# First loads dealt over two queues, 20 warming products in place of 27, and the input's squares in four wide pinned instructions, in a hybrid decoder layer

## The chip, the core and the metric

The kernel runs on one core of one Trainium2 chip. The metric is the device time of one execution in microseconds (us). Three runs of the kernel before took 1563.19, 1560.8 and 1563.22 us; their median is 1563.19 us. The profile was taken from one more execution of 1562.6 us, whose span from the first instruction to the last is 1560.7 us.

## The reference

The kernel computes one layer of a decoder on 256 tokens of width 2048, in float32, with weights read from memory:

```python
u = rms_norm(h, pre_mix_gain, 1e-6)          # u = x * rsqrt(mean(x*x) + eps) * gain
z = u @ w_in                                 # 2048 x 14336
zq, zk, zv, zc, zga, zgc = split(z)
...                                          # differential attention on zq, zk, zv
zc = zc + glu_bias
c_val, c_gate = split(zc, 2)
c = c_val * sigmoid(c_gate)
c = causal_depthwise_conv(c, dw_kernel, dw_bias)     # 31 taps
c = silu(layer_norm(c)); conv_out = c @ w_conv_out + b_conv_out
m = sigmoid(zga) * attn_out + sigmoid(zgc) * conv_out
h = h + rms_norm(m @ w_out, post_mix_gain)
f = square(relu(rms_norm(h, pre_ff_gain) @ w_ff1)) @ w_ff2
return h + rms_norm(f, post_ff_gain)
```

The first norm matters here. The factor rsqrt(mean(x*x) + eps) is one number per token, so it can be applied behind the product with `w_in`: the kernel multiplies x by the gain alone, starts the products, and scales the sums later.

## The kernel before

**Chunks.** All weights come in chunks of 128 x 2048 float32 (1 MiB), in one fixed order: first the 32 chunks of the convolution branch, in pairs of one value chunk (`w_cv`) and one gate chunk (`w_cg`), then q, k, v, the gates, the output projections and the feed-forward layer. Each chunk is loaded into a buffer `raw` (three buffers) by a DMA that SyncE issues (line 97), rounded to a high half `wh` by ScalarE (line 103) and to a low half `wl`, raw minus `wh`, by VectorE (line 109). `wh` and `wl` have three buffers each, so a chunk's halves can be written once TensorE has done with those of the chunk three places before. A `raw` buffer is free for its next load when the chunk's `wl` is written.

**Products.** TensorE works through a pair of chunks in `ws_pair`: for each chunk 16 products of `wh` with the activations' two halves side by side (512 columns, line 180), then 16 of `wl` with the high half (256 columns, line 182). A pair fills one of two PSUM tiles `ps`. ScalarE copies one part of the sum out (line 187) into `z`, VectorE adds the rest (line 188), and then the PSUM tile is free for the pair after the next. `z` has two buffers.

**The lead.** The first pair (chunks 0 and 1, raw tiles `lead[0]` and `lead[1]`) is done in pieces, so that TensorE can start early: x (2 MiB, transposed, tile `xt`) and the two chunks are loaded in parts, and for each of four groups j of four k-tiles ScalarE writes the high halves of x times gain (line 157) and of the weights, VectorE the low halves (lines 158 and 109), and TensorE does lines 168 and 171 for each k-tile and chunk. All this is pinned in the written order. Before it TensorE runs `WARM` products of the identity with itself (line 293), which leave no result.

**The norm's factor.** Lines 325 to 341 square x (ScalarE, 16 instructions of 128 x 256), add the squares up in `xss` (VectorE, 15 additions), sum over partitions with a product with ones (lines 336 and 340, on TensorE), and take square root and reciprocal: `rb` (per column) and `rt` (per token). `xt` and `xss` live in a pool that is closed behind this. `rb` is needed when the first pair's `z` is scaled (line 384); behind that come the sigmoid (line 385), the gated value `c` (line 388) and the filter (lines 369 and 373). The third pair's `z` can be written only when the first pair's `c` is done, since `z` has two buffers.

**Order.** Instructions that are pinned (`pin`) keep the written order among themselves; the rest are placed on each engine by a scheduler that estimates a timeline and takes priorities (`tc.high_priority`). At run time each engine runs its own list strictly in order, and waits on semaphores where an operand isn't there. A DMA signals on one of eight counters in turn, so the ninth one waits for the landing of the one that had its counter.

Of the kernel before, what the change touches and what calls it, by code (L numbers as in the profile page):

```python
# [11 lines left out]
F32 = mybir.dt.float32  # L12
F32R = mybir.dt.float32r
AF = mybir.ActivationFunctionType
ALU = mybir.AluOpType
# [3 lines left out]
P = 128  # L19
S = 256  # L20
NT = S // P
D = 2048
KT = D // P
# [16 lines left out]
CONV_LATE = 4000  # L40
CHAIN = 400
CHAINS = 2
WARM = 27
AHEAD = 3
LAG = 4
EARLY = 3
# [6 lines left out]
def tile_layer(ctx, tc, x, x_t, pre, vecs, lams, rope_t, subln, b_conv, post_mix, post_ff,  # L53
               w_q, w_k, w_v, w_cv, w_cg, w_ga, w_gc, w_co, w_o, w_f1, w_f2, out):
    nc = tc.nc
# [25 lines left out]
    pin = tc.keep_in_program_order  # L81

    def load(pieces):
        i = state["next"]
        state["next"] += 1
        state["live"] += 1
        chunk = (rawp.tile([P, CHUNK], F32, name="raw"), whp.tile([P, CHUNK], F32R, name="wh"),
                 wlp.tile([P, CHUNK], F32R, name="wl"))
        for j in range(pieces):
            load_part(chunk, i, j, pieces)  # L90
        queue.append(chunk[1:])
        return chunk

    def load_part(chunk, i, j, pieces, pinned=False, eng=None):
        w = CHUNK // pieces
        sl = slice(j * w, (j + 1) * w)
        a = (eng or nc.sync).dma_start(chunk[0][:, sl], order[i][:, sl])
        if pinned:
            pin(a)
# [117 lines left out]
    def rsqrt(dst, src, eps_tile, scale=1.0):  # L217
        nc.scalar.activation(dst, src, AF.Sqrt, bias=eps_tile, scale=scale)
        nc.vector.reciprocal(dst, dst)
# [4 lines left out]
    def aux_ps():  # L224
        tag = XT[xi[0] % 4]
        xi[0] += 1
        return psx.tile([P, 512], F32, name="aux", tag=tag)
# [30 lines left out]
    xsp = xst.enter_context(tc.tile_pool(name="xsp", bufs=1))  # L258
    xt = xsp.tile([P, KT, S], F32, name="xt")
    gpre = const.tile([P, KT], F32, name="gpre")  # L260
    lead = [load(0) for i in range(2)]

    def load_x(a, b):
        pin(nc.sync.dma_start(xt[:, a:b], x_t[:, a:b]))

    load_x(0, 2)
    pin(nc.scalar.dma_start(gpre, pre))
    load_part(lead[0], 0, 0, 4, pinned=True)
    load_part(lead[1], 1, 0, 4, pinned=True, eng=nc.scalar)
    load_x(2, 4)  # L270
    for j in range(1, 4):
        load_x(4 * j, 4 * j + 4)
        load_part(lead[0], 0, j, 4, pinned=True)
        load_part(lead[1], 1, j, 4, pinned=True, eng=nc.scalar)
    epsn = const.tile([P, 1], F32, name="epsn")
    nc.vector.memset(epsn, NORM_EPS)
    warm = const.tile([P, 1], F32, name="warm")
# [3 lines left out]
    ones = const.tile([P, P], F32, name="ones")  # L281
# [9 lines left out]

    for i in range(WARM):
        pin(nc.tensor.matmul(aux_ps()[:, 0:P], ident, ident, start=True, stop=True))
# [28 lines left out]
    def vcol(ct, r):  # L322
        return vec[:, ct, r:r + 1]

    xss = xsp.tile([P, S], F32, name="xss")
    for k in range(KT):
        if k == 0:
            nc.scalar.activation(xss, xt[:, k], AF.Square)
        else:
            sq = xsp.tile([P, S], F32, name="xsq", bufs=2)  # L330
            nc.scalar.activation(sq, xt[:, k], AF.Square)
            nc.vector.tensor_tensor(xss, xss, sq, op=ALU.add)
    rb = const.tile([P, S], F32, name="rb")
    rt = const.tile([P, NT], F32, name="rt")
    pb = aux_ps()[:, 0:S]
    nc.tensor.matmul(pb, ones, xss, start=True, stop=True)
    rsqrt(rb, pb, epsn, 1.0 / D)
    pc = aux_ps()[:, 0:NT]
    for t in range(NT):
        nc.tensor.matmul(pc[:, t:t + 1], xss[:, t * P:(t + 1) * P], ones[:, 0:1], start=True, stop=True)  # L340
    rsqrt(rt, pc, epsn, 1.0 / D)
    xst.close()
    rb2 = rb.unsqueeze(1).to_broadcast([P, 2, S])

# [160 lines left out]
    for j in range(4):  # L505
        yj = y_all[:, 4 * j:4 * j + 4]
        nc.vector.tensor_tensor(yj, yj, acc1.unsqueeze(1).to_broadcast([P, 4, S]), op=ALU.subtract)
        for ct in range(4 * j, 4 * j + 4):
            if ct == 0:
                nc.scalar.activation(acc2, y_all[:, ct], AF.Square)  # L510
            else:
                sq = tmpp.tile([P, S], F32, name="sq")
# [24 lines left out]
    for n in range(NB):  # L537
# [7 lines left out]
        for j in (2 * n, 2 * n + 1):  # L545
            pt = aux_ps()
            for i in range(2):
                k = 2 * j + i
# [19 lines left out]
    for n in range(NB):  # L568
        ps = as_block(ma, apart=(n == NB - 1))
        ns = slice(n * 512, (n + 1) * 512)  # L570
        with tc.high_priority(offset=CHAIN if n == NB - 1 else 0):
            for t in range(NT):
                sq = fin2.tile([P, 512], F32, name="fsq")
# [61 lines left out]
    for q in range(NQ):  # L635
# [9 lines left out]
        for n in range(NB):  # L645
            ps = as_block(ga, stagger=(q == NQ - 1 and n == NB - 1), apart=(q == NQ - 1 and n == NB - 1))
            ns = slice(n * 512, (n + 1) * 512)
            for t in range(NT):
# [5 lines left out]
                if q == NQ - 1:  # L654
                    last = n == NB - 1
                    with tc.high_priority(offset=CHAIN if last else 0):
                        sq = fin2.tile([P, 512], F32, name="fsq")
# [81 lines left out]
```

## Time and profile before

| what | value |
|---|---|
| median of three runs | 1563.19 us (1560.8 to 1563.22) |
| profiled execution | 1562.6 us, span 1560.7 us |
| TensorE (PE) busy | 1543.0 us, 99% of the span |
| VectorE (DVE) busy | 1118.0 us, 72% |
| ScalarE (ACT) busy | 719.7 us, 46% |
| TensorE's mean granted clock | 0.995 of full speed |
| DMA | 296.86 MB, mean 190 GB/s |

TensorE is busy nearly all the time, and the chain of work that ended last is TensorE for 97% of the span. So time can be taken from this kernel only where TensorE idles or runs at the lower clock, and those places are few; the list of what TensorE waited for shows them, and the timelines of the first 65 us show what stands around them. "PEld" is TensorE's loading of weights, which runs beside its products; a float32 product appears as two records.

### The profile page before, as it was taken

Reading aid. Unit: us, or ns where it says so; the run is one execution under the profiler, and the core shown is the slowest. Engines: PE = TensorE matmul, PEld = TensorE weight load, DVE = VectorE, ACT = ScalarE, POOL = GpSimd, SP = SyncE. Lnnn points to the kernel's source line nnn. Section 1 sums busy time; section 2 is a strip of 40 time slices with the busy share of each in tenths; the row PEclk is TensorE's granted clock in tenths of the full one; section 3 lists DMA queues with packets and bytes.
Section 4 is the critical chain, followed back from the end, with each engine's and each line's share of the span. In section 5 each row is a group of like instructions: output and inputs, shape, how many; then the busy total and the mean of one; then the engine's idle time right before and its main releaser. Section 6 shows DMA issues by size and latency. Waiting matters only on the chain.

```text
span 1560.7 us, 19198 instructions
## 1 busy us (share of the span) xinstructions
PE 1543.0 (99%) x7844; PEld 1319.0 (85%) x7844; DVE 1118.0 (72%) x1409; ACT 719.7 (46%) x755; POOL 5.2 (0%) x28
## 2 busy tenths in 40 slices
PE   9999999999999999999999999999999999999997
PEld 8788888888888888888887888888888888888886
DVE  7899999999999997956546764456554665456554
ACT  7444454645555545733435543444433443344442
POOL 0000000000000000000000000000000000000000
PEclk9999999999999999999999999999999999999999
DMA  7555555454545555555654654555555555555552
GB/s 286 195 191 189 189 189 188 165 187 162 189 162 185 195 197 195 196 187 182 266 193 147 234 189 175 200 199 189 188 190 194 190 189 185 191 211 189 174 200 84
DMA packets 45143, 296.86 MB, mean 190 GB/s; under 512 B 5120, under 2 KB 5248, under 8 KB 10368
## 3 DMA queue, kind: packets, MB, share of 16 engines
q1 hardware_dynamic: 43632, 289.34, 51.3%
q0 software_dynamic: 704, 5.24, 0.8%
q10 hardware_dynamic: 720, 1.06, 0.2%
q8 instruction: 61, 1.00, 0.2%
q14 instruction: 26, 0.21, 0.0%
HBM read 293.53 MB, written 2.10 MB: 189 GB/s over the span
## 4 chain that ended last, share of the span: by engine, by line
PE 97%; DVE 1%; DMA 1%; ACT 0%; issue 0%; DVEq 0%; ACTq 0%
PE ps L180 29%; PE ps L197 16%; PE ps L198 16%; PE ps L196 16%; PE ps L182 15%; PE ps L168 1%; DMA raw<-in_w_cv_dram 1%; PE po L456 1%; PE ps L171 1%; PE s L428 0%; PE aux L197 0%; PE aux L196 0%; PE aux L198 0%; DVE y_sb L672 0%; PE aux L236 0%; PE s L427 0%
## 5 line engine op out<-in xcount | busy, mean ns | idle before, releaser
L109 DVE TENSOR_TENSOR wl<-raw,wh 128x2048 fp32r<-128x2048 f32 (+2 forms) x292 | 625.3, 2145 | 376.4 <-ACT wh L103 372.0
L103 ACT CAST wh<-raw 128x2048 fp32r<-128x2048 f32 (+2 forms) x292 | 522.2, 1793 | 717.6 <-PE ps L198 342.2
L180 PE MATMUL ps<-act,wh 128*128 128x512 f32 x1984 | 480.5, 393 | 3.6 <-DVE z L188 3.6
L180 PEld LDWEIGHTS ps<-act,wh 128*128 128x128 f32 x1984 | 365.7, 189 | 74.4 <-issue 3.7
L182 PEld LDWEIGHTS ps<-act,wl 128*128 128x128 f32 x1984 | 256.5, 191 | 10.0
L182 PE MATMUL ps<-act,wl 128*128 128x256 f32 x1984 | 264.0, 284 | 0.0
L196 PE MATMUL ps<-wh,act 128*128 128x512 f32 x624 | 243.7, 391 | 0.0
L198 PE MATMUL ps<-wh,act 128*128 128x512 f32 x624 | 243.7, 390 | 0.0
L197 PE MATMUL ps<-wl,act 128*128 128x512 f32 x624 | 243.5, 390 | 0.0
L373 DVE SCALAR_TENSOR_TENSOR y_all<-c,vec,y_all 128x256 f32<-128x256 f32 x480 | 209.9, 482 | 0.0
L196 PE MATMUL ps<-wh,g 128*128 128x512 f32 x496 | 193.0, 389 | 0.0
L197 PE MATMUL ps<-wl,g 128*128 128x512 f32 x496 | 193.0, 389 | 0.0
L198 PE MATMUL ps<-wh,g 128*128 128x512 f32 x496 | 192.9, 389 | 0.0
L198 PEld LDWEIGHTS ps<-wh,act 128*128 128x128 f32 x624 | 117.1, 188 | 24.1
L196 PEld LDWEIGHTS ps<-wh,act 128*128 128x128 f32 x624 | 117.2, 188 | 24.0
L197 PEld LDWEIGHTS ps<-wl,act 128*128 128x128 f32 x624 | 117.2, 188 | 23.9
L198 PEld LDWEIGHTS ps<-wh,g 128*128 128x128 f32 x496 | 93.1, 188 | 19.4
L196 PEld LDWEIGHTS ps<-wh,g 128*128 128x128 f32 x496 | 93.1, 188 | 19.3
L197 PEld LDWEIGHTS ps<-wl,g 128*128 128x128 f32 x496 | 93.1, 188 | 19.1
L188 DVE TENSOR_TENSOR z<-z,ps 128x512 f32<-128x512 f32 x64 | 43.6, 681 | 0.0
L187 ACT COPY z<-ps 128x512 f32<-128x512 f32 x64 | 37.4, 586 | 2.5 <-PE ps L182 1.6
L653 DVE TENSOR_TENSOR y_sb<-ps,y_sb 128x512 f32<-128x512 f32 x23 | 14.9, 687 | 20.1 <-PE ps L198 20.1
(170 smaller groups left out, 700.9 us busy)
## 6 DMA issues: line engine op xcount, KB each, us to landing
raw<-in_w_f_dram SPq DMA_DIRECT2D x124, 1024.0 KB, 4.8
raw<-in_w_q_dram SPq DMA_DIRECT2D x16, 1024.0 KB, 4.8
raw<-in_w_k_dram SPq DMA_DIRECT2D x16, 1024.0 KB, 4.8
raw<-in_w_v_dram SPq DMA_DIRECT2D x16, 1024.0 KB, 4.8
raw<-in_w_ga_dram SPq DMA_DIRECT2D x16, 1024.0 KB, 4.9
raw<-in_w_gc_dram SPq DMA_DIRECT2D x16, 1024.0 KB, 4.8
raw<-in_w_co_dram SPq DMA_DIRECT2D x16, 1024.0 KB, 4.8
raw<-in_w_o_dram SPq DMA_DIRECT2D x16, 1024.0 KB, 4.9
```

Source lines behind the costliest of these rows:

```text
L103: i = nc.scalar.copy(wh[:, a:b], raw[:, a:b])
L109: i = (eng or nc.vector).tensor_sub(wl[:, a:b], raw[:, a:b], wh[:, a:b].bitcast(F32))
L168: a = nc.tensor.matmul(ps, wh[:, sl], acts.both(k), start=(k == 0), stop=False)
L171: b = nc.tensor.matmul(ps[:, S:], wl[:, sl], acts.hi(k), start=False, stop=(k == KT - 1))
L180: nc.tensor.matmul(ps[:, j], wh[:, k * P:(k + 1) * P], acts.both(k), start=(k == 0), stop=False)
L182: nc.tensor.matmul(ps[:, j, S:], wl[:, k * P:(k + 1) * P], acts.hi(k), start=False, stop=(k == KT - 1))
L187: nc.scalar.copy(dst, ps[:, :, S:])
L188: nc.vector.tensor_tensor(dst, dst, ps[:, :, 0:S], op=ALU.add)
L196: nc.tensor.matmul(ps, acts.hi(k, a, b), wh[:, sl], start=(k == 0), stop=False)
L197: nc.tensor.matmul(ps, acts.hi(k, a, b), wl[:, sl], start=False, stop=False)
L198: nc.tensor.matmul(ps, acts.lo(k, a, b), wh[:, sl], start=False, stop=(k == KT - 1))
L373: i = nc.vector.scalar_tensor_tensor(y, c[:, j:j + S], vcol(ct, V_DW + j), y, op0=ALU.mult, op1=ALU.add)
```

## The change

Three edits. `WARM` goes from 27 to 20. The first loads are issued in another order: the first quarter of the gate chunk, the gains `gpre` and x's k-tiles 4 to 7 on ScalarE's queue, everything else of x and the two chunks on SyncE's queue in the order in which the groups j need it (before, all four quarters of the gate chunk were on ScalarE's queue). And the squares of x are four instructions of 128 x 1024 with three additions of that width and two folding ones, all pinned and with a priority raised by `CHAIN` (400), as are the products and roots behind them.

```diff
-WARM = 27
+WARM = 20
...
+    def load_x(a, b, eng=None):
+        pin((eng or nc.sync).dma_start(xt[:, a:b], x_t[:, a:b]))
+    def load_w(i, j, eng=None):
+        load_part(lead[i], i, j, 4, pinned=True, eng=eng)
     load_x(0, 2)
+    load_w(1, 0, nc.scalar)
+    load_w(0, 0)
     pin(nc.scalar.dma_start(gpre, pre))
-    load_part(lead[0], 0, 0, 4, pinned=True)
-    load_part(lead[1], 1, 0, 4, pinned=True, eng=nc.scalar)
     load_x(2, 4)
-    for j in range(1, 4):
+    load_x(4, 8, nc.scalar)
+    load_w(0, 1)
+    load_w(1, 1)
+    for j in range(2, 4):
         load_x(4 * j, 4 * j + 4)
-        load_part(lead[0], 0, j, 4, pinned=True)
-        load_part(lead[1], 1, j, 4, pinned=True, eng=nc.scalar)
+        load_w(0, j)
+        load_w(1, j)
...
-    xss = xsp.tile([P, S], F32, name="xss")
-    for k in range(KT):
-        if k == 0:
-            nc.scalar.activation(xss, xt[:, k], AF.Square)
-        else:
-            sq = xsp.tile([P, S], F32, name="xsq", bufs=2)
-            nc.scalar.activation(sq, xt[:, k], AF.Square)
-            nc.vector.tensor_tensor(xss, xss, sq, op=ALU.add)
...
+    xss = xsp.tile([P, 4, S], F32, name="xss")
+    with tc.high_priority(offset=CHAIN):
+        for j in range(4):
+            sq = xsp.tile([P, 4, S], F32, name="xsq", bufs=2) if j else xss
+            pin(nc.scalar.activation(sq, xt[:, 4 * j:4 * j + 4], AF.Square))
+            if j:
+                pin(nc.vector.tensor_tensor(xss, xss, sq, op=ALU.add))
+        pin(nc.vector.tensor_tensor(xss[:, 0:2], xss[:, 0:2], xss[:, 2:4], op=ALU.add))
+        pin(nc.vector.tensor_tensor(xss[:, 0], xss[:, 0], xss[:, 1], op=ALU.add))
...
```

On SyncE's queue this is the start of the list before. `xt` is x, `raw` the chunks, a part of 128 x 512 a quarter chunk or two k-tiles of x:

```order
L264 DMA xt<-in_x_t_dram 128x512
L97 DMA raw<-in_w_cv_dram 128x512
L264 DMA xt<-in_x_t_dram 128x512
L264 DMA xt<-in_x_t_dram 128x1024
L97 DMA raw<-in_w_cv_dram 128x512
L264 DMA xt<-in_x_t_dram 128x1024
L97 DMA raw<-in_w_cv_dram 128x512
L264 DMA xt<-in_x_t_dram 128x1024
L97 DMA raw<-in_w_cv_dram 128x512
L97 DMA raw<-in_w_cv_dram 128x2048
```

And this is the start of the same queue's list now:

```order
L264 DMA xt<-in_x_t_dram 128x512
L97 DMA raw<-in_w_cv_dram 128x512
L264 DMA xt<-in_x_t_dram 128x512
L97 DMA raw<-in_w_cv_dram 128x512
L97 DMA raw<-in_w_cg_dram 128x512
L264 DMA xt<-in_x_t_dram 128x1024
L97 DMA raw<-in_w_cv_dram 128x512
L97 DMA raw<-in_w_cg_dram 128x512
L264 DMA xt<-in_x_t_dram 128x1024
L97 DMA raw<-in_w_cv_dram 128x512
L97 DMA raw<-in_w_cg_dram 128x512
L97 DMA raw<-in_w_cv_dram 128x2048
```

The second quarters of both chunks now stand fourth and fifth; x's k-tiles 4 to 7 have left this queue, and three quarters of the gate chunk have joined it.

On TensorE, around the products that sum the squares (line 336 before, 343 now), the list before is this, from the fifth and sixth chunk on:

```order
L180 MATMUL ps<-act,wh 128x512 x16
L182 MATMUL ps<-act,wl 128x256 x4
L336 MATMUL aux<-xss,ones 128x256
L340 MATMUL aux<-ones,xss 128x1 x2
L182 MATMUL ps<-act,wl 128x256 x12
L180 MATMUL ps<-act,wh 128x512 x16
```

Now it is this, where the first row is of the sixth chunk's low half and the next of the seventh's high half:

```order
L182 MATMUL ps<-act,wl 128x256 x16
L180 MATMUL ps<-act,wh 128x512 x10
L343 MATMUL aux<-xss,ones 128x256
L346 MATMUL aux<-ones,xss 128x1 x2
L180 MATMUL ps<-act,wh 128x512 x6
L182 MATMUL ps<-act,wl 128x256 x16
```

The sums stood behind 4 of the sixth chunk's 16 low products; they now stand behind all 16 and 10 more of the seventh chunk.

On VectorE, from the reciprocals of the norm's factor to the addition (line 188) that frees the PSUM tile for the ninth chunk, the list before is this (`wl` rows are chunks, lines 369 and 373 the filter):

```order
L219 RECIPROCAL rb<-rb 128x256
L219 RECIPROCAL rt<-rt 128x2
L109 TENSOR_TENSOR wl<-raw,wh 128x2048
L384 TENSOR_TENSOR z<-z,rb 128x512 x2
L391 TENSOR_TENSOR rope_sb<-rope_sb,rb 128x512
...
L109 TENSOR_TENSOR wl<-raw,wh 128x2048
L388 SCALAR_TENSOR_TENSOR c<-z,vec 128x256
...
L373 SCALAR_TENSOR_TENSOR y_all<-c,vec,y_all 128x256 x3
L109 TENSOR_TENSOR wl<-raw,wh 128x2048
L373 SCALAR_TENSOR_TENSOR y_all<-c,vec,y_all 128x256
L188 TENSOR_TENSOR z<-z,ps 128x512
```

Now the same stretch is this:

```order
L219 RECIPROCAL rb<-rb 128x256
L219 RECIPROCAL rt<-rt 128x2
L391 TENSOR_TENSOR z<-z,rb 128x512 x2
L109 TENSOR_TENSOR wl<-raw,wh 128x2048
L395 SCALAR_TENSOR_TENSOR c<-z,vec 128x256 x2
L398 TENSOR_TENSOR rope_sb<-rope_sb,rb 128x512
L412 TENSOR_SCALAR sub_333<-sub_333 128x256
L406 TENSOR_TENSOR sq<-lam_in 128x256
L376 TENSOR_SCALAR y_all<-c,vec 128x256 x2
L188 TENSOR_TENSOR z<-z,ps 128x512
```

Three `wl` rows stood between the reciprocals and that addition; one does now, and the scaling of `z` follows the reciprocals at once. On ScalarE a copy out of PSUM (line 187) now stands right behind the two first sigmoids; before, a `wh` rounding stood between them. In the lead no square and no addition of squares is left on either engine.

## Rows read from the trace of the kernel before

**Rows 1.** Waits of TensorE over the whole run: us in all, times, longest.

```profile
PE ps L180 <- DVE z L188: 3.6, 1, 3.6
...
PE ps L168 <- ACT wh L103: 1.3, 1, 1.3
```

**Rows 2.** Timeline of TensorE, 0 to 45 us: start, us, instruction.

```profile
16.90 0.63 PE L168 MATMUL ps<-act,wh 128*128 128x512 f32 x1
...
17.54 0.63 PE L168 MATMUL ps<-act,wh 128*128 128x512 f32 x1
...
24.72 0.39 PE L168 MATMUL ps<-act,wh 128*128 128x512 f32 x1
...
25.07 3.83 PE L180 MATMUL ps<-act,wh 128*128 128x512 f32 x16
...
30.65 3.82 PE L180 MATMUL ps<-act,wh 128*128 128x512 f32 x16
```

**Rows 3.** Stretches: us, busy PE, PEld, DVE, ACT, POOL, clock, DMA share, GB/s.

```profile
9.70:12.40 2.70, 2.70 (x17) 2.38 (x17) 1.80 (x5) 2.21 (x6) 0.00 (x0) 1.00 1.04 410
...
18.00:19.50 1.50, 1.50 (x7) 1.30 (x6) 1.50 (x5) 1.50 (x5) 0.00 (x0) 0.50 0.36 147
...
63.00:66.00 3.00, 2.94 (x9) 2.37 (x10) 3.00 (x7) 0.57 (x2) 0.00 (x0) 0.66 0.85 319
```

**Rows 4.** Timeline of TensorE, 38 to 85 us.

```profile
45.91 0.59 PE L336 MATMUL aux<-xss,ones 128*128 128x256 f32 x2
...
57.43 2.07 PE L182 MATMUL ps<-act,wl 128*128 128x256 f32 x16
...
63.06 5.50 PE L180 MATMUL ps<-act,wh 128*128 128x512 f32 x16 [3.55 <-DVE z L188]
```

**Rows 5.** Chain of waits, 0 to 64 us: start, us, what.

```profile
3.92 9.42 DMA raw<-in_w_cv_dram
...
57.68 1.93 ACT wh L103
...
59.63 2.29 DVE wl L109
...
62.31 0.61 DVE z L188
```

**Rows 6.** Timeline of TensorE's weight loads, 7 to 8 us: warming products.

```profile
6.85 1.31 PEld L293 LDWEIGHTS aux<-ident 128*128 128x128 f32 x11
```

**Rows 7.** Timeline of ScalarE, 0 to 45 us.

```profile
9.85 0.91 ACT L157 ACTIVATE act<-xt,gpre 128x256 fp32r<-128x256 f32 x2 [0.74 <-DMA xt<-in_x_t_dram]
...
12.02 0.51 ACT L157 ACTIVATE act<-xt,gpre 128x256 fp32r<-128x256 f32 x1 [0.33 <-DMA xt<-in_x_t_dram]
...
13.36 1.14 ACT L103 CAST wh<-raw 128x512 fp32r<-128x512 f32 x2 [0.83 <-DMA raw<-in_w_cv_dram]
```

**Rows 8.** Timeline of VectorE, 0 to 45 us.

```profile
16.41 0.42 DVE L332 TENSOR_TENSOR xss<-xss,xsq 128x256 f32<-128x256 f32 x1
...
17.50 1.29 DVE L109 TENSOR_TENSOR wl<-raw,wh 128x512 fp32r<-128x512 f32 x2
...
18.70 1.67 DVE L158 SCALAR_TENSOR_TENSOR act<-xt,gpre,act 128x256 fp32r<-128x256 f32 x4
```

**Rows 9.** Timeline of ScalarE, 38 to 85 us.

```profile
53.99 1.28 ACT L385 ACT_TABLE_LOAD   x1
...
55.29 0.91 ACT L385 ACTIVATE z<-z,vec 128x256 f32<-128x256 f32 x2
```

**Rows 10.** Timeline of VectorE, 38 to 85 us.

```profile
47.94 1.75 DVE L219 RECIPROCAL rb<-rb 128x256 f32<-128x256 f32 x1 [3.61 <-ACT rb L218]
...
51.82 1.29 DVE L384 TENSOR_TENSOR z<-z,rb 128x512 f32<-128x512 f32 x2
...
53.03 0.68 DVE L391 TENSOR_TENSOR rope_sb<-rope_sb,rb 128x512 f32<-128x512 f32 x1
```

More of the change, by code (lines that the diff above doesn't have):

```diff
@@ L261, in tile_layer @@
     lead = [load(0) for i in range(2)]
-    def load_x(a, b):
-        pin(nc.sync.dma_start(xt[:, a:b], x_t[:, a:b]))
+    def load_x(a, b, eng=None):
+        pin((eng or nc.sync).dma_start(xt[:, a:b], x_t[:, a:b]))
+    def load_w(i, j, eng=None):
+        load_part(lead[i], i, j, 4, pinned=True, eng=eng)
     load_x(0, 2)
+    load_w(1, 0, nc.scalar)
+    load_w(0, 0)
     pin(nc.scalar.dma_start(gpre, pre))
-    load_part(lead[0], 0, 0, 4, pinned=True)
-    load_part(lead[1], 1, 0, 4, pinned=True, eng=nc.scalar)
     load_x(2, 4)
-    for j in range(1, 4):
+    load_x(4, 8, nc.scalar)
+    load_w(0, 1)
+    load_w(1, 1)
+    for j in range(2, 4):
         load_x(4 * j, 4 * j + 4)
-        load_part(lead[0], 0, j, 4, pinned=True)
-        load_part(lead[1], 1, j, 4, pinned=True, eng=nc.scalar)
+        load_w(0, j)
+        load_w(1, j)
     epsn = const.tile([P, 1], F32, name="epsn")
@@ L323, in vcol @@
         return vec[:, ct, r:r + 1]
-    xss = xsp.tile([P, S], F32, name="xss")
-    for k in range(KT):
-        if k == 0:
-            nc.scalar.activation(xss, xt[:, k], AF.Square)
-        else:
-            sq = xsp.tile([P, S], F32, name="xsq", bufs=2)
-            nc.scalar.activation(sq, xt[:, k], AF.Square)
-            nc.vector.tensor_tensor(xss, xss, sq, op=ALU.add)
     rb = const.tile([P, S], F32, name="rb")
     rt = const.tile([P, NT], F32, name="rt")
[L335 to L341, printed above, removed]
+    xss = xsp.tile([P, 4, S], F32, name="xss")
[7 more added lines that the diff above has]
+        pin(nc.vector.tensor_tensor(xss[:, 0], xss[:, 0], xss[:, 1], op=ALU.add))
+        pb = aux_ps()[:, 0:S]
+        nc.tensor.matmul(pb, ones, xss[:, 0], start=True, stop=True)
+        pc = aux_ps()[:, 0:NT]
+        for t in range(NT):
+            nc.tensor.matmul(pc[:, t:t + 1], xss[:, 0, t * P:(t + 1) * P], ones[:, 0:1], start=True, stop=True)
+        rsqrt(rb, pb, epsn, 1.0 / D)
+        rsqrt(rt, pc, epsn, 1.0 / D)
     xst.close()
```

## The prediction

> **What bounds the kernel now.** I read three views, from coarse to fine. The list of what TensorE waited for comes first: it is short, and two of its entries lie where the change is, 3.6 us for VectorE's addition into `z` and 1.3 us for ScalarE's rounding in the lead [rows 1]. So the kernel is bound by TensorE, and the change can only work through these waits and through the clock. The table of stretches comes second: the granted clock is 0.50 of full speed, the 1.2 GHz level, from 18.0 to 19.5 and 0.66 on the mean from 63 to 66, and 1.00 between 9.7 and 12.4 [rows 3]; both dips follow the two waits. Last the timelines. In the lead TensorE's step of one wide and one narrow product takes 17.54 - 16.90 = 0.64 us in the dip and 25.07 - 24.72 = 0.35 us outside it, and the third chunk (the first one behind the lead) starts at 25.07 [rows 2]. The ninth chunk could have started at 57.43 + 2.07 = 59.50; it started at 63.06, and its 16 wide products took 5.50 us [rows 4] in place of 3.82 [rows 2]: the wait cost 3.55 us, the clock behind it 1.68.
>
> What set the lead is the landing of the second quarters. ScalarE waited for x's k-tiles 2 and 3 until 9.85, for k-tiles 4 to 7 until 12.02, and for the value chunk's second quarter until 13.36 [rows 7]; that DMA was issued at 3.92 and took 9.42 us [rows 5], since it stood fifth in SyncE's queue with three more quarters of the gate chunk coming through ScalarE's.
>
> **The lead, part by part.** *Order of the loads.* By 12.02 SyncE's queue had landed its first four loads, 1.25 MiB, while the other queue ran beside it. Now the first five loads of SyncE's queue are 1.25 MiB too, and the fifth is the last second quarter; so group 1 is complete at about 12.0 in place of 13.36. X's k-tiles 4 to 7 end the 0.75 MiB of the other queue, which has no more than that beside it; I take them as there by 12.0 too. Afterwards one queue alone carries 1 MiB a group; at the 410 GB/s of 9.7 to 12.4 [rows 3] that is 2.6 us, so groups 2 and 3 are complete at 14.6 and 17.2.
>
> *VectorE in the lead.* Group 1 costs half of 1.14 us for the gate quarter's rounding [rows 7], 0.65 for its low half and three of four remainders of 1.67 us [rows 8]: 12.0 + 0.57 + 0.65 + 1.25 = 14.5. Each further group is 1.29 + 1.67 us less the overlap between instructions, 2.8 (18.70 - 17.50 = 1.2 for the first pair) [rows 8]. That ends at about 20.1. The squares that stood between are gone: one addition of 0.42 us [rows 8] for each, about one in every group here.
>
> *TensorE in the lead.* Of the 32 steps, 24 belong to groups 1 to 3. From about 13.3, when the gate quarter's low half is there, they take 24 x 0.35 = 8.4 us: 21.7 at full clock, 1.6 behind VectorE, so TensorE itself is the later. But its first four k-tiles now arrive spaced, with idle time of 2 us and more before 13.3, and such idle time was followed by half clock before. A dip as long as the one before, about 3.4 us, costs 3.4 / 0.64 = 5.3 steps in the time of 9.7, so 4.4 x 0.35 = 1.5 us. Part of it can fall where TensorE has nothing to do; I take 1.0 of 1.5, and the third chunk at 22.7. Gain 25.07 - 22.7 = 2.4 us; bounds 3.4 (no dip) and 0 (TensorE done no earlier).
>
> *Fewer warming products.* Seven products are 14 records of 1.31 / 11 = 0.12 us [rows 6]: TensorE is free 1.6 us earlier, at about 8.0. That is worth nothing by itself, since group 1's landing and not the warming sets the lead; its price is in the idle time above.
>
> *The gains behind the gate quarter.* `gpre` now stands second in ScalarE's queue, and nothing can start without it. Its bounds: no delay, or landing only with x's k-tiles 4 to 7 behind it at 12.0, which would start group 0 there and end the lead some 3 us later than forecast, at 25.7. It is tiny and second in line, so I take no delay.
>
> **The squares and the wait for the ninth chunk.** The wide squares and additions are not in this trace: each ScalarE one lies between a 128x256 step (about 0.5 us, half of 0.91) [rows 9] and a 128x2048 rounding (1.93) [rows 5], each addition between 0.42 [rows 8] and 2.29 [rows 5]. I take the middle, 1.05 and 1.2, as widths of 1024 lie halfway to 2048. They are off the path either way: the order puts the last folding addition behind the eighth chunk's low half, which waits until TensorE has finished the fifth chunk, three chunks of 30.65 - 25.07 = 5.58 us [rows 2] behind the lead. That is 16.7 + 2.3 + 0.4 = 19.4 us behind the lead's end; the product that sums them (line 343) comes at 4 x 5.58 and 10 wide products of 3.82 / 16 = 0.24 [rows 2]: 24.7. With the upper bounds some 3 us of the 5 us of cover are used; beyond that every us is TensorE's, as the product stands in its queue in order.
>
> From that product the factor's chain runs. Before, it was issued at 45.91 and the ninth chunk was released at 63.06 [rows 4]: 17.15 us. The chain's last links were ScalarE's rounding of the eleventh chunk, 1.93 us from 57.68, the copy of `z` queued behind it, VectorE's `wl` of 2.29 and then the addition [rows 5]. Now, counted from the product's issue: 0.65 until the sum is there, 0.5 for the root, 1.75 and 0.1 for the reciprocals, 1.29 for scaling both `z` [rows 10], so 4.3. On ScalarE the tenth chunk's rounding waits for the seventh's wide products (0.8 for the summing products and 6 x 0.24: 2.2) and ends at 4.2, the table load takes 1.28 and the first sigmoid half of 0.91 [rows 9]: 6.0. VectorE does the tenth chunk's `wl` from 4.3 to 6.5, both `c` to 7.4, and then the five short instructions for the rotary table, the lambda products and two filter starts: 0.6 [rows 10] and four of some 0.35, to 9.4. The addition of 0.61 [rows 5] ends at 10.0, the release is 10.1. TensorE wants it later by less than before: it had 59.50 - 45.91 = 13.6 us of work between, and the product now stands 12 narrow products (2.07 / 16 each [rows 4]) and 10 wide ones further back, 1.5 + 2.4 us, so 9.7. The wait is 0.4 us in place of 3.55, and I expect no dip behind it: 3.1 + 1.7 = 4.8 us gained. Bounds: none left (5.2) and a wait of 1.3 us with its dip, as short a wait as the lead's [rows 1], which leaves a gain of 2.2.
>
> The sum, against the profiled execution: 1562.6 - 2.4 - 4.8 = 1555.4 us. That execution is 0.6 under the median of the runs shown; I make no correction for that.
>
> **Rules that speak against it.** TensorE's clock came back from 0.5 in the lead after it had worked without a gap [rows 2, 3]. The Trainium skill ("TensorE: Matmul & The Clock Gate", section on the clock gate) says that half rate is the default and activity releases it; by that alone fewer warming products could leave the whole lead slow, and this is the second rival below. The queues: beside ScalarE's loads the chunk's second quarter took 9.42 us [rows 5]. The Trainium skill ("DMA: Bandwidth & Descriptors", section on issuing engines not being separate queues) says that issuing from several engines saves only issue time; by it the deal over queues brings no bandwidth, and what remains is the order, the first rival's ground.
>
> **Rivals.**
> 1. *The loads land no earlier* (0.18): SyncE's queue now carries three quarters more, and bytes are only exchanged, or `gpre` is late. For it: the engines were fully loaded from 9.7 on [rows 3]. Against it: what is exchanged is what was not needed yet. Lead end at 25.1, stall gone: 1562.6 - 4.8 = 1557.8.
> 2. *The clock stays at half for the lead* (0.11): the 24 steps at 0.64 end at 13.3 + 15.4 = 28.7, 3.6 later than now; 1562.6 + 3.6 - 4.8 = 1561.4. Against it: in the dip before, steps without a gap brought the clock back.
> 3. *The factor's chain is as long as before* (0.09): the summing product is further back in TensorE's queue, so the same 17.15 us would make the ninth chunk wait 17.15 - 9.7 = 7.4 us, 3.9 more than now: 1562.6 + 3.9 - 2.4 = 1564.1, slower; with a lead that gains nothing, 1566.5. It decides from a chain of 9.7 + 3.55 + 2.4 = 15.6 us. Against it: two of three `wl` and one rounding have left the chain in the new order.
>
> **How the numbers follow.** The forecast holds 0.62, with 1553 to 1557.5 of its own: 1562.6 - 3.4 - 5.2 = 1554.0 at its best, with one us for the spread of the runs shown. The range of 8 in 10 reaches down to 1552.8 and up to 1560, which takes in rival 1 and part of 2. About 0.2%, 3.1 us, is what a measurement here can tell from no change. Faster by more than that (under 1560.1): the forecast, rival 1 and a quarter of rival 2, 0.83. Slower (over 1566.3): half of rival 3, 0.04. Between: 0.13.
>
> **What would show it.** Right: group 1's rounding starts near 12.0 and TensorE's first chunk behind the lead near 22.7; no squares among the lead's instructions; the summing product some 24.7 us behind the lead's end without a wait; the ninth chunk within 0.5 us of the eighth's end and 3.82 us for its wide products. Wrong: a second quarter landing at 13 or later (1), clock 0.50 over more than about 4 us of the lead (2), or a wait of several us on line 188 again (3). Any new wait of TensorE behind 65 us, where there is hardly any now, would break the sum altogether.

## The result and the profile after

Six runs of the changed kernel have a median of 1553.74 us (1552.41 to 1554.0), six of the kernel before 1562.76 us. The ratio is 0.9942, 95% interval 0.9929 to 0.9955: a gain of 9.0 us where 7.2 were forecast. The profiled execution took 1552.62 us, its span 1550.9, against 1560.7 before; it is one of the two quickest of the six, 1.1 us under their median, so the traces show a little more gain than the medians.

First the list of what TensorE waited for in the changed kernel, over the whole run, as in [rows 1]:

```profile
PE aux L299 <- POOL ident masks.py:199: 1.6, 1, 1.6
PE aux L236 <- DVE h_sb L592: 1.5, 2, 1.3
PE ps L168 <- DVE act L158: 0.4, 1, 0.4
```

Both entries of [rows 1] are gone: no wait for `z` on line 188 and none for a rounding on line 103. The first row here is the start of the warming, the other two lie at the mixing stage.

The timeline of TensorE, with two steps of the lead and the four places that answer to [rows 2, 4] (start, us, instruction):

```profile
13.36 0.39 PE L168 MATMUL ps<-act,wh 128*128 128x512 f32 x1
...
20.42 0.40 PE L168 MATMUL ps<-act,wh 128*128 128x512 f32 x1
...
20.82 3.93 PE L180 MATMUL ps<-act,wh 128*128 128x512 f32 x16
...
45.50 0.59 PE L343 MATMUL aux<-xss,ones 128*128 128x256 f32 x2
...
53.39 2.07 PE L182 MATMUL ps<-act,wl 128*128 128x256 f32 x16
55.57 3.87 PE L180 MATMUL ps<-act,wh 128*128 128x512 f32 x16
```

The third chunk starts at 20.82 in place of 25.07, 4.25 us earlier. The summing product comes 45.50 - 20.82 = 24.7 us behind it, as forecast. The eighth chunk's low half ends at 53.39 + 2.07 = 55.46 and the ninth chunk starts at 55.57: 0.1 us of wait in place of 3.55, and 3.87 us for its 16 wide products in place of 5.50.

The same profile by stretches, with the columns of [rows 3]:

```profile
9.70:12.40 2.70, 2.69 (x15) 2.09 (x14) 2.70 (x7) 2.70 (x8) 0.00 (x0) 1.00 1.04 413
18.00:19.50 1.50, 1.50 (x10) 1.32 (x10) 1.22 (x4) 0.79 (x2) 0.00 (x0) 1.00 0.76 142
55.50:59.50 4.00, 3.93 (x18) 3.33 (x19) 4.00 (x6) 0.60 (x2) 0.00 (x0) 1.00 0.23 98
...
830.00:850.00 20.00, 18.20 (x103) 15.12 (x104) 15.05 (x34) 15.44 (x42) 0.56 (x1) 1.00 0.31 112
```

The granted clock is 1.00 in the lead and at the ninth chunk; both dips of [rows 3] have gone. The last row is the mixing stage, to be compared with this row of the kernel before:

```profile
830.00:850.00 20.00, 18.09 (x85) 14.45 (x84) 14.25 (x28) 11.77 (x31) 0.56 (x1) 0.91 0.49 179
```

So the 9.8 us between the two spans add up. The ninth chunk's high half ended at 63.06 + 5.50 = 68.56 [rows 4] and now ends at 55.57 + 3.87 = 59.44: 9.1 us earlier, of which 4.25 come from the lead and 4.9 from what follows: the wait and the slow products take 5.1 us less, and 0.2 us are lost on the way to them. The remaining 0.7 us come later than that. The mixing stage's clock, 0.91 on the mean of 20 us before and 1.00 here, is the one difference that I found there. The twelve profiles of this document bear it out: from the ninth chunk's low half to the end of the span, the five that show 1.00 in these 20 us take 1491.1 to 1491.7 us, the seven that show 0.91 take 1492.3 to 1493.4. Kernels with and without the change are among both, so I don't count it as the change's.

What filled the lead: VectorE's timeline, with [rows 8, 10] before.

```profile
7.82 0.48 DVE L158 SCALAR_TENSOR_TENSOR act<-xt,gpre,act 128x256 fp32r<-128x256 f32 x1 [6.77 <-ACT act L157]
...
17.95 1.27 DVE L158 SCALAR_TENSOR_TENSOR act<-xt,gpre,act 128x256 fp32r<-128x256 f32 x3
...
34.81 1.22 DVE L339 TENSOR_TENSOR xss<-xss,xsq 128x1024 f32<-128x1024 f32 x1
...
41.55 0.42 DVE L341 TENSOR_TENSOR xss<-xss 128x256 f32<-128x256 f32 x1
...
54.75 0.68 DVE L188 TENSOR_TENSOR z<-z,ps 128x512 f32<-128x512 f32 x1
...
56.46 2.28 DVE L109 TENSOR_TENSOR wl<-raw,wh 128x2048 fp32r<-128x2048 f32 x1
```

Between the first two rows no row of VectorE has a wait; it is done with the lead at 17.95 + 1.27 = 19.2. The wide additions lie behind the lead, 1.22 us each, and the last fold is done at 41.97, 3.5 us before TensorE needs it. The last two rows matter for what follows: the third pair's sum into `z` stands ahead of the eleventh chunk's `wl`.

ScalarE's timeline, with [rows 7, 9] before:

```profile
7.28 0.51 ACT L157 ACTIVATE act<-xt,gpre 128x256 fp32r<-128x256 f32 x1 [3.64 <-DMA gpre<-in_pre_dram]
...
10.52 1.13 ACT L103 CAST wh<-raw 128x512 fp32r<-128x512 f32 x2
...
18.86 1.91 ACT L103 CAST wh<-raw 128x2048 fp32r<-128x2048 f32 x1 [0.71 <-DMA raw<-in_w_cv_dram]
...
27.81 1.05 ACT L337 ACTIVATE xss<-xt 128x1024 f32<-128x1024 f32 x1
```

Group 1's rounding starts at 10.52 without a wait (forecast 12.0, 13.36 before). But the lead now starts on the gains: ScalarE waits 3.64 us for `gpre`, until 7.28. The third chunk's rounding waits for its load until 18.86 and is done at 18.86 + 1.91 = 20.77, just when TensorE is through with the lead: the third chunk could not have started earlier unless this load came earlier too. A wide square takes 1.05 us.

The issues of the two loads that the forecast turned on (engine, KB each, us from issue to landing):

```profile
raw<-in_w_cg_dram SPq DMA_DIRECT2D x1, 256.0 KB, 8.0
gpre<-in_pre_dram ACTq DMA_DIRECT2D x1, 8.0 KB, 6.0
```

The first is the gate chunk's second quarter, the last of group 1: issued at 2.60, so there at 10.6. The gains were issued at 1.18.

### The profile page after: what moved, and what is told of

It is laid out like the page before. It is cut to its first block, busy times and chain, and to the rows that moved or that the text cites. A ratio compares the mean times of both kernels' runs of the same rounds, so it can differ in the third digit from the quotient of the medians.

```text
span 1550.9 us, 19142 instructions
## 1 busy us (share of the span) xinstructions
PE 1537.6 (99%) x7830; PEld 1314.2 (85%) x7830; DVE 1116.3 (72%) x1399; ACT 717.4 (46%) x743; POOL 5.1 (0%) x28
## 4 chain that ended last, share of the span: by engine, by line
PE 99%; DVE 1%; ACT 0%; issue 0%; POOL 0%; DVEq 0%; ACTq 0%; POOLq 0%
PE ps L180 29%; PE ps L196 16%; PE ps L197 16%; PE ps L198 16%; PE ps L182 15%; PE ps L168 1%; PE po L463 1%; PE ps L171 1%; PE s L435 0%; PE aux L299 0%; PE aux L197 0%; PE aux L196 0%; PE aux L198 0%; DVE y_sb L679 0%; PE s L434 0%; PE aux L557 0%
## 5 line engine op out<-in xcount | busy, mean ns | idle before, releaser
L182 PEld LDWEIGHTS ps<-act,wl 128*128 128x128 f32 x1984 | 256.6, 191 | 10.1
L196 PEld LDWEIGHTS ps<-wh,g 128*128 128x128 f32 x496 | 93.1, 188 | 19.2
L660 DVE TENSOR_TENSOR y_sb<-ps,y_sb 128x512 f32<-128x512 f32 x23 | 14.9, 686 | 20.1 <-PE ps L198 20.1
```

Source lines behind the costliest of these rows:

```text
L182: nc.tensor.matmul(ps[:, j, S:], wl[:, k * P:(k + 1) * P], acts.hi(k), start=False, stop=(k == KT - 1))
L196: nc.tensor.matmul(ps, acts.hi(k, a, b), wh[:, sl], start=(k == 0), stop=False)
```

## The experiments

Each compares with runs of the kernel before on the same chip (medians 1562.2 to 1562.4); the ratio is the time over theirs, with its 95% interval. The first four edit the kernel before, the others the changed kernel. A trace is of one execution, and small differences in the lead are not safe: the same 27 warming products took from 7.88 to 9.16 us in the six profiled executions that have them.

**1. The order of the loads alone.** The `dma_start` lines of the change, with 27 warming products and the narrow squares.

```diff
...
-    for j in range(1, 4):
+    load_x(4, 8, nc.scalar)
+    load_w(0, 1)
+    load_w(1, 1)
+    for j in range(2, 4):
...
```

> The kernel before with the new order of the first loads alone (27 warming products, narrow squares). Theory (the lead is gained by the second quarters landing earlier): VectorE still adds squares in the lead, so the third chunk starts at about 21.5 us in place of 25.07, with no half clock in the lead. The new times also move the scheduler's order: the eleventh chunk's low half no longer stands ahead of the third pair's sum, so no wait at the ninth chunk. Together about 1554 us. Rival (the lead is gained mostly by taking the squares out of it): third chunk at 23.5 to 25, total 1556 to 1558. Rival (the ninth chunk's wait hangs on the wide squares): the wait of 3.5 us and its dip stay, total about 1559.

Measured: 1555.42 us, ratio 0.9954 (0.9939 to 0.9968). Its rows of TensorE and then of VectorE:

```profile
22.85 3.80 PE L180 MATMUL ps<-act,wh 128*128 128x512 f32 x16
...
57.10 3.82 PE L180 MATMUL ps<-act,wh 128*128 128x512 f32 x16
```

```profile
19.14 0.43 DVE L338 TENSOR_TENSOR xss<-xss,xsq 128x256 f32<-128x256 f32 x1
...
54.41 0.68 DVE L188 TENSOR_TENSOR z<-z,ps 128x512 f32<-128x512 f32 x1
...
57.36 2.29 DVE L109 TENSOR_TENSOR wl<-raw,wh 128x2048 fp32r<-128x2048 f32 x1
```

The loads' order alone takes 2.2 us out of the lead, and it alone also ends the wait for the ninth chunk: 7.0 of the 9.0 us. VectorE works without a gap here too, but six narrow additions stand ahead of its last remainder of the lead, at some 0.35 us of its time each: 2.1 us, and the third chunk starts 22.85 - 20.82 = 2.0 us later than in the changed kernel, 1.7 us later than in experiment 6, which has the same 27 warming products.

**2. The wide pinned squares alone.** The change's block of `xss` (lines 333 to 348) in the kernel before.

```diff
+    with tc.high_priority(offset=CHAIN):
+        for j in range(4):
+            sq = xsp.tile([P, 4, S], F32, name="xsq", bufs=2) if j else xss
+            pin(nc.scalar.activation(sq, xt[:, 4 * j:4 * j + 4], AF.Square))
...
```

> The kernel before with the wide, pinned squares with priority alone. In its order on VectorE the eleventh chunk's low half still stands ahead of the third pair's sum, though the factor's chain has lost a low half. Theory (order: that low half waits for TensorE's eighth chunk, and TensorE's ninth waits for the sum behind it): a wait of about 3.4 us at the ninth chunk and 1.7 us of half clock stay; the lead gains 0 to 1 us, since the second quarters land as before; total 1562 us. Rival (length: a shorter chain from the summing product to the sum ends the wait, as the prediction reckoned): no wait, total about 1557 us.

Measured: 1563.39 us, ratio 1.0006 (0.9996 to 1.0015). TensorE, then VectorE:

```profile
25.47 3.80 PE L180 MATMUL ps<-act,wh 128*128 128x512 f32 x16
...
63.78 5.51 PE L180 MATMUL ps<-act,wh 128*128 128x512 f32 x16 [3.85 <-DVE z L188]
```

```profile
60.35 2.29 DVE L109 TENSOR_TENSOR wl<-raw,wh 128x2048 fp32r<-128x2048 f32 x1 [0.51 <-ACT wh L103]
...
62.95 0.68 DVE L188 TENSOR_TENSOR z<-z,ps 128x512 f32<-128x512 f32 x1
```

Nothing is gained. The lead still waits for its loads, and the wait for `z` with its slow products stays, 3.85 us. The two VectorE rows show why: the eleventh chunk's `wl` stands ahead of the sum. That chunk reuses the eighth chunk's buffers, so its `wl` can't start before TensorE has finished with the eighth, and the sum that frees TensorE is stuck behind it.

**3. 20 warming products alone.**

```diff
-WARM = 27
+WARM = 20
```

> The kernel before with 20 warming products alone. Theory of the prediction (worth nothing by itself, group 1's landing sets the lead): TensorE starts the lead at about 8.3 us with gaps, third chunk at 24.5 to 25.1, total 1562.8 within 1 us. Rival (the idle time before 13.3 us brings the half clock earlier, where less work is, or longer): third chunk at 23.5 or at 26 and later, total 1561 or 1564 us.

Measured: 1563.39 us, ratio 1.0004 (0.9995 to 1.0013). Alone the seven products are worth nothing, as the theory has it. The third chunk starts at 25.15, and TensorE's row of the ninth chunk is that of before:

```profile
63.13 5.50 PE L180 MATMUL ps<-act,wh 128*128 128x512 f32 x16 [3.55 <-DVE z L188]
```

**4. Only the order on VectorE and ScalarE.** A dependency that orders and waits for nothing puts the eleventh chunk's rounding and `wl` behind the third pair's copy and sum; loads, squares and warming are those of before.

```diff
...
+                if late:
+                    for i, first in zip((hi, lo), third_sum):
+                        tc.add_manual_dep(i.ins, first.ins.name, order_only, reason="third pair's sum first")
...
```

> The kernel before with one thing more: the eleventh chunk's two halves are made to stand behind the third pair's copy and sum on ScalarE and VectorE, by an order without a semaphore; nothing else is changed, the summing product stands where it stood. Theory (order): the sum is done near 58.6 us, before TensorE wants the ninth chunk at 59.5; no wait and no half clock behind it, total 1562.8 - 5.2 = 1557.6 us. Rival (length: the factor comes too late): the wait stays at 2 us or more, total above 1560 us.

Measured: 1555.81 us, ratio 0.9959 (0.9945 to 0.9973). TensorE, then VectorE:

```profile
45.59 0.59 PE L345 MATMUL aux<-xss,ones 128*128 128x256 f32 x2
...
59.03 3.82 PE L188 MATMUL ps<-act,wh 128*128 128x512 f32 x16
```

```profile
57.49 0.69 DVE L196 TENSOR_TENSOR z<-z,ps 128x512 f32<-128x512 f32 x1
...
60.20 2.30 DVE L112 TENSOR_TENSOR wl<-raw,wh 128x2048 fp32r<-128x2048 f32 x1
```

The ninth chunk starts at 59.03 without a wait and at full clock, though the summing product stands where it stood before (45.59 against 45.91 [rows 4]) and the loads are untouched. So the order of these two instructions is the cause of the wait, and the squares' place is not. It is 1.8 us faster than expected. By the trace, 1.2 us of its gain lie behind the ninth chunk, in an execution whose mixing stage shows the clock at 1.00, and 0.3 us in the lead (third chunk at 24.75); neither is the order's.

**5. The changed kernel with 27 warming products.**

```diff
-WARM = 20
+WARM = 27
```

> The changed kernel with 27 warming products again. Theory of the prediction (worth nothing by itself): third chunk at 20.8 to 21.1 us, total 1553.7 to 1554.1 us. Rival (once the loads come early, TensorE's start counts): TensorE is held until 9.6 in place of 8.46, third chunk near 22, total 1554.9 us.

Measured: 1560.81 us, ratio 0.9993 (0.9983 to 1.0002): 7 us lost with seven small products. TensorE, then VectorE:

```profile
22.62 3.92 PE L180 MATMUL ps<-act,wh 128*128 128x512 f32 x16 [0.79 <-ACT wh L103]
...
60.74 5.51 PE L180 MATMUL ps<-act,wh 128*128 128x512 f32 x16 [3.55 <-DVE z L188]
```

```profile
57.32 2.29 DVE L109 TENSOR_TENSOR wl<-raw,wh 128x2048 fp32r<-128x2048 f32 x1 [0.21 <-ACT wh L103]
...
59.92 0.68 DVE L188 TENSOR_TENSOR z<-z,ps 128x512 f32<-128x512 f32 x1
```

The rival foresaw the third chunk's delay, but neither theory the wait. The `wl` stands ahead of the sum again: nothing in that code differs, so the list scheduler, which places instructions by its own estimate of when each can start, decided the other way. Why its estimate turns here is not shown. The wait and its clock cost 5 us, and the third chunk started 1.8 us later.

**6. The same, with the order of experiment 4 forced.** The diffs of 4 and 5 together in the changed kernel.

> The changed kernel with 27 warming products, as in e4, and the eleventh chunk's two halves made to stand behind the third pair's copy and sum, as in e8. Theory (order; the seven warming products cost their time only by the order that the scheduler makes of them): third chunk at 22 to 22.7 us as in e4, no wait at the ninth chunk, total 1560.8 - 5.2 = 1555.6 us. Rival (seven more products cost TensorE itself several us): total above 1558 us.

Measured: 1553.93 us, ratio 0.995 (0.9932 to 0.9968). TensorE, then VectorE:

```profile
21.13 3.85 PE L188 MATMUL ps<-act,wh 128*128 128x512 f32 x16
```

```profile
54.16 0.68 DVE L196 TENSOR_TENSOR z<-z,ps 128x512 f32<-128x512 f32 x1
```

With the order fixed the seven products cost 21.13 - 20.82 = 0.3 us in the lead, less than expected, and the time is that of the changed kernel. The wait was the order's. The rest of experiment 5's loss was in its lead: the warming ended at 10.73 there and at 9.99 here, and ScalarE waited for the third chunk's load until 20.66 there and until 18.79 here, which cost TensorE 0.79 us. Why both came later in that execution is open.

**7. The gains first.** `gpre` ahead of the gate quarter in ScalarE's queue.

```diff
+    pin(nc.scalar.dma_start(gpre, pre))
     load_w(1, 0, nc.scalar)
     load_w(0, 0)
-    pin(nc.scalar.dma_start(gpre, pre))
```

> The changed kernel with the gains' load ahead of the gate chunk's first quarter on ScalarE's queue, nothing else. Theory (VectorE is busy without a gap from its first low half at 7.82 to the lead's end, so its start sets the lead, and the gains' landing at 7.2 sets its start): gains at about 4 us, first low half of x at 5, VectorE done with the lead near 18.4, third chunk at 19.8 to 20.1, total about 1552.9 us. Rival (the value chunk's first quarter at 7.0 holds the lead anyway): third chunk at 20.6 or later, total 1553.7 us.

Measured: 1554.15 us, ratio 0.995 (0.9935 to 0.9965); the third chunk at 22.98, not at 20. ScalarE's rows:

```profile
3.96 0.51 ACT L157 ACTIVATE act<-xt,gpre 128x256 fp32r<-128x256 f32 x1 [0.31 <-DMA gpre<-in_pre_dram]
...
8.36 0.30 ACT L103 CAST wh<-raw 128x128 fp32r<-128x128 f32 x1 [0.70 <-DMA raw<-in_w_cg_dram]
...
18.53 0.62 ACT L103 CAST wh<-raw 128x512 fp32r<-128x512 f32 x1 [0.68 <-DMA raw<-in_w_cg_dram]
```

The gains are there 3.3 us earlier, but now ScalarE waits for the gate chunk's first quarter until 8.36 and for its fourth until 18.53. The expectation failed. It also left out the third chunk, whose high half is ready only at 20.77 in the changed kernel. The four executions took from 1553.03 to 1556.5 us and the profiled one 1554.8, so this lead is not that of all four.

**8. All big loads on one queue.** The same order of need, all on SyncE's queue; only the gains on ScalarE's.

```diff
-    load_w(1, 0, nc.scalar)
     load_w(0, 0)
+    load_w(1, 0)
...
-    load_x(4, 8, nc.scalar)
+    load_x(4, 8)
```

> The changed kernel with all loads of x and of the two chunks on SyncE's queue, in the order of need; the gains alone on ScalarE's. Theory (the order of need is what counts, the second queue only saves issue time): the gate chunk's second quarter lands within 0.7 us of the changed kernel's 10.6, third chunk at 20.3 to 21.3, total within 0.6 us of 1553.7. Rival (one queue draws less from the engines at the start): that quarter at 12 us or later, third chunk at 22 to 23, total 1555 to 1556 us.

Measured: 1554.34 us, ratio 0.9949 (0.9932 to 0.9966). TensorE's row of the third chunk:

```profile
21.62 3.91 PE L180 MATMUL ps<-act,wh 128*128 128x512 f32 x16 [0.31 <-ACT wh L103]
```

The time is within 0.6 us, as the theory has it; the third chunk, at 21.62, lies between the theory's range and the rival's. One queue does nearly what two do. The order in which the parts are asked for is most of what the change is worth there, the dealing over two queues 0.8 us of the lead at most.

**9. The wide squares left free.** The changed kernel without the pins and the priority (the products and roots behind the squares had only the priority, and lose it too).

```diff
-    with tc.high_priority(offset=CHAIN):
+    if True:
...
-            pin(nc.scalar.activation(sq, xt[:, 4 * j:4 * j + 4], AF.Square))
+            nc.scalar.activation(sq, xt[:, 4 * j:4 * j + 4], AF.Square)
```

> The changed kernel with the wide squares neither pinned nor with priority. The scheduler then puts three additions and a folding one between the lead's instructions on VectorE, and the summing product into the third chunk. Theory (in the lead VectorE is the bound now, each addition there costs its length): 3 x 1.2 + 0.6 us more on VectorE, third chunk at 24 to 25 us, no wait at the ninth chunk, total 1557 us. Rival (the additions fall into gaps of VectorE): third chunk under 22, total 1554 to 1555 us.

Measured: 1557.78 us, ratio 0.9971 (0.996 to 0.9982). TensorE, VectorE and a stretch of the lead:

```profile
24.97 3.62 PE L180 MATMUL ps<-act,wh 128*128 128x512 f32 x15
```

```profile
12.73 1.22 DVE L339 TENSOR_TENSOR xss<-xss,xsq 128x1024 f32<-128x1024 f32 x1 [0.46 <-ACT xsq L337]
```

```profile
16.00:19.50 3.50, 3.50 (x13) 3.02 (x12) 3.50 (x7) 3.50 (x8) 0.00 (x0) 0.52 0.31 129
```

As expected, three such additions fall back into the lead, TensorE runs short of work there, the clock goes to 0.52, and the lead's gain of 4.25 us is gone but for 0.1. So the pins and the priority together, not the width, carry the squares' part of the gain; no run takes the two apart.

**10. The gains on GpSimd's queue, with the sum first.** A try at a faster kernel: the order dependency of experiment 4 in the changed kernel, and

```diff
-    pin(nc.scalar.dma_start(gpre, pre))
+    pin(nc.gpsimd.dma_start(gpre, pre))
```

> The changed kernel with the gains loaded through GpSimd's queue, and with the third pair's copy and sum first, as in e8 (without that the scheduler puts the eleventh chunk's low half ahead again). Theory (VectorE sets the lead from its first low half on): gains there by 5 us, the gate chunk's first quarter as early as now (4.6), VectorE's chain starts at 7.2 with one low half of x already done, third chunk at 19.8 to 20.2 us, no wait at the ninth chunk, total about 1552.9 us. Rival (the loads land later, as they did in e5): third chunk at 21 to 23 us, total 1554 to 1556 us.

Measured: 1555.13 us, ratio 0.9955 (0.9939 to 0.9971): the rival's price. The row of its DMA issues (KB, median us to landing), TensorE's ninth chunk, a stretch with it, and VectorE's row behind the reciprocals:

```profile
gpre<-in_pre_dram POOLq DMA_DIRECT2D x1, 8.0 KB, 6.7
```

```profile
57.56 3.87 PE L188 MATMUL ps<-act,wh 128*128 128x512 f32 x16 [1.62 <-DVE z L196]
```

```profile
60.00:64.00 4.00, 4.00 (x27) 3.64 (x26) 4.00 (x7) 1.91 (x1) 0.00 (x0) 1.00 0.29 96
```

```profile
50.42 0.29 DVE L422 TENSOR_SCALAR sub<-sub 128x256 f32<-128x256 f32 x1 [2.47 <-DMA sub<-in_subln_dram]
```

Issued at 1.23, the gains landed at 7.9 from this queue as well, later than in the changed kernel, and the third chunk starts at 21.44. But the loss isn't the lead's alone. The ninth chunk waits 1.62 us though the sum stands first: the scheduler put the scaling of `sub` ahead of that of `z`, and VectorE stood 2.47 us for its load there. In experiment 6 the same two rows stand in this order without a wait, and the ninth chunk has none; no run takes this wait out here. No version measured is faster than the changed kernel.

## Why the prediction was right, and where it was not

- **Group 1 complete at 12.0: too late,** it was there at 10.6. The forecast took the rate of the kernel before for granted. From 2 to 9.7 us the DMA engines moved 270, 185, 319 and 400 GB/s in stretches of 2, 2, 2 and 1.7 us, before 246, 145, 266 and 341. By 10.6 that makes 2.64 MB, which the kernel before had moved by 11.4; so, as an estimate, the rate is worth 0.8 of the 1.4 us, and the rest is that fewer bytes of later groups came first. The engines were busy about as much (shares of 0.92, 0.73, 0.92 and 1.03, before 0.90, 0.75, 0.87 and 0.96); why the rate is higher with this order stays open.
- **The lead's gain of 2.4: mis-sized, 4.25 measured,** past its upper bound of 3.4. Two terms failed. The loads were earlier by 1.4 us, so VectorE was done at 19.2 and not 20.1. And the 1.0 us set aside for a half-clock dip did not come: TensorE was busy for 3.89 us of 3.90 from 8.5 on and 3.59 of the next 3.60, and the clock stayed at 1.00. TensorE then ends 1.6 us behind VectorE, as forecast. So the landings no longer limit the lead. At its end TensorE does, with steps of (20.42 - 13.36) / 20 = 0.353 us on end, and close behind it stand VectorE's own 11.4 us of work and the third chunk's load. Experiment 1 shows how close: 2.1 us more on VectorE made the lead 1.7 us longer at the same warming, and that is why the squares had to leave it too. The loads alone gave 2.2 us, the squares alone nothing, both together 25.07 - 21.13 = 3.9 (experiment 6), and with the shorter warming 4.25.
- **`gpre` second in line, no delay: wrong.** Its 8 KB took 6.0 us and held ScalarE until 7.28. It cost little, since the value chunk's first quarter, issued at 1.19, also landed only at 7.0. Experiment 7 took the delay away and gained nothing; experiment 10 did not take it away.
- **The squares off the path: right.** 1.05 us for a square and 1.22 for an addition were measured, 1.05 and 1.2 forecast; the summing product comes 24.7 us behind the lead's end without a wait. Experiment 9 is the price when the squares are not kept behind the lead: 4.0 us.
- **The wait of 0.4 in place of 3.55, and no dip: right, by the forecast's own walk.** From the summing product's issue to the release it counted 10.1 us; 55.57 - 45.50 = 10.07 was measured, and the links on the way agree (both `z` scaled after 4.2 us, 4.3 forecast; both `c` after 7.5, 7.4 forecast), so the number is not luck. TensorE wanted it 55.46 - 45.50 = 10.0 us behind it (9.7 forecast), so 0.1 is left. The 4.8 us gained stand against 4.9. What the forecast did not see is where this came from. It had the new order before it, took it as given, and put the gain under the squares. The squares alone leave the wait at 3.85 (experiment 2), the loads alone end it (1), and so does the order alone (4). Every profile with a wait of 3.55 us or more has the eleventh chunk's `wl` ahead of the third pair's sum, and none with the sum first has one; but sum first does not ensure that nothing waits, as the 1.62 us of experiment 10 show. The order is a by-product of the scheduler's estimate.
- **Fewer warming products, "worth nothing by itself": right in the kernel before (3), wrong as a part of this change.** TensorE's own time for them is 0.3 us (6), yet the changed kernel with 27 of them has the order turned round and is 7 us slower (5).
- **Rival 1, loads no earlier:** fell, 10.52 for group 1's rounding. **Rival 2, half clock for the lead:** fell here, but it is what experiment 9 shows over a part of it. **Rival 3, the chain as long as before:** fell for this kernel. What the prediction held against it, the new order, is what was missing in experiments 2 and 5; there the chain from the summing product to the ninth chunk took 15.8 and 15.5 us and the wait 3.85 and 3.55, not its 17.15 and 7.4, since the `wl` in the way is tied to the eighth chunk and not to the summing product.

## What to carry to other kernels

On an in-order engine, look at what stands ahead of the instruction that frees the bottleneck's buffer: a preparation step tied to the bottleneck's own progress there makes it wait for itself, and one order-only dependency took 6.6 us off this kernel without any other change (5.4 of them by the trace at the ninth chunk). Where a list scheduler sets the order, an edit that is worth nothing in its own time (seven small products) can cost 5 us by turning two instructions round, so compare the order before arguing from durations, and pin the pair that matters. When loads are brought forward, ask what is late next: here the loads, VectorE's squares and then TensorE's own steps with the third chunk's load limited the lead one behind the other, and only the first two edits together gave the gain.

## What the runs showed of the hardware

- The 8 KB of gains took 6.0 us from issue to landing when issued second in ScalarE's queue, 6.7 us from GpSimd's queue, and 3.2 us when issued first in ScalarE's queue at 0.73 (the kernel before and experiment 7); a 256 KB quarter issued first there took 3.9. Its small size did not make it fast beside the big loads; its place in the queue changed its time.
- The length of one wait of TensorE did not settle what the clock did behind it. Those of 3.55 to 3.85 us were each followed by products at half clock (5.50 us for 16 in place of 3.82), and one of 1.62 us left it at 1.00 (experiment 10). But the shorter wait of the lead before, 1.3 us with small gaps behind it, was followed by 0.50 [rows 1, 3], and the mixing stage's longest wait, 1.24 to 1.27 us in all twelve profiles, was followed by a lower clock in seven and not in five.
- A square of 128x1024 took 1.05 us on ScalarE, one of a quarter of that width 0.40 in the kernel before (the row below), so width alone takes a third off ScalarE's time for squares; on VectorE an addition of 1024 took 1.22 against 0.42 for 256 [rows 8].

```profile
19.27 0.40 ACT L331 ACTIVATE xsq<-xt 128x256 f32<-128x256 f32 x1
```
